# A DeltaNet layer: decays computed ahead of the keys, Q's norms read back from DRAM, gates stored from another queue, one exponential per head

## The chip, the core and the metric

The kernel runs on one core of one Trainium2 chip. Its time is device microseconds for one execution; lower is better. One profiled execution of the same program gives the page and the trace that are quoted below.

## What is computed

A two-layer decoder trunk on 528 tokens (16 meta tokens and 512 real ones) of width 1024, in float32: a retention layer, a SwiGLU feed-forward layer, a gated DeltaNet layer and another feed-forward layer, each with a norm ahead of it and a residual addition. The change touches the DeltaNet layer alone. Its core, for each of 8 heads (chunk by chunk):

```python
qkv = silu(causal_conv(h @ w_in, conv_w))          # 4 taps
q = l2norm(q) * DN_DK ** -0.5;  k = l2norm(k)
beta = sigmoid(beta_in);  g = -exp(a_log) * softplus(a_in + dt_bias)
gam = cumsum(g)                                    # inside a chunk
decay = exp(where(i >= j, gam_i - gam_j, -inf))
a_mat = where(i > j, beta * (k @ k.T) * decay, 0)
u, w = solve(eye + a_mat, [v * beta, k * beta * exp(gam)])
v_new = u - w @ state
o = (q * exp(gam)) @ state + ((q @ k.T) * decay) @ v_new
state = state * exp(g_last) + (k * exp(g_last - gam)).T @ v_new
out = (rmsnorm(o) * silu(gate)) @ w_out
```

## The kernel before

Matrix products keep float32 accuracy by splitting both operands into a rounded high part and a remainder: `hi*hi + hi*lo + lo*hi`, three matmuls for one (`mm3`, L470). A weight block of 128x1024 is loaded by SyncE's queue (`wraw`, L173), its high part is cast by ScalarE (`whi`, L179), and the remainder is formed by VectorE (`wlo`, L180). `gemm` multiplies one such block with all 528 tokens: 48 matmuls of 128x264 into one of two accumulator tiles `g` (two PSUM banks each). Smaller products use four one-bank tiles `m`.

The program is written in one thread of Python with a clock of its own: `tick()` advances it by one step after each k-block of a gemm (six matmuls), and generators that were given to `spawn` with a delay are resumed between matmuls when their step has come; `yield n` asks to be resumed n steps later, `next(gen)` and `finish(gen)` run one at once. The order in which each engine's queue then holds its instructions is set when the program is built. It follows the program's order by priority, but an instruction that is planned to be ready earlier can go ahead of one written before it. On the chip each queue runs in that fixed order.

The DeltaNet layer (`deltanet`, from about 780 us) has these stages:

- Head 0's two key/query gemms (`gemm_pair`), with the row norms `rb` made meanwhile.
- `dn_gates` (L1213): 32 matmuls with the 16 columns of beta and a (L1235, 48 rows of output because of the splitting), ten small transposing matmuls (L1252), a chain of small VectorE and ScalarE operations for beta and softplus, cumulative sums (L1292), and the matrix of decays. For each pair of heads, `rows_in` broadcasts the sums from DRAM into `dec`, GpSimd adds a mask of 1e30 (L1356), and ScalarE takes `exp(-x + sum)` of each 128x128 chunk, four for a head (L1363). It yields between parts (`GATE_STEPS`, `ROWS_IN`, `MASKED`).
- `dn_keys` for each head (L1366): a gemm for K and one for Q. `conv_evac` (L1198) multiplies by `rb` into one of two `pad` buffers (VectorE, L1202), takes the four taps (ScalarE L1205, VectorE L1207), and a Silu (L1210). The result is stored to DRAM (`d_kq`) and split into `z`. For Q, `dn_norms` is spawned: four transposes (L1396), four squares with a row sum (ScalarE, L1400), one small operation (L1402).
- `dn_attention` for each head: K'K and K'Q products, beta and decay applied (L1446), stored to `d_mp`. It needs its pair's decays, and runs `dn_gates` on until they are there.
- `dn_inverse`: forward substitution on VectorE for all heads together, while TensorE multiplies value weights (`dn_values`) and two heads' gate weights (`dn_silu_gate`).
- `dn_states`: the recurrence, pair by pair, among the remaining value, gate and output gemms. The silu'd gates are stored to DRAM (`d_sg`, L1608) and read back when their head is finished (L1695).

ScalarE's Exp and Silu are in different tables; the trace shows an `ACT_TABLE_LOAD` wherever one follows the other.

Of the kernel before, what the change touches and what calls it, by code (L numbers as in the profile page):

```python
# [10 lines left out]
AF = mybir.ActivationFunctionType  # L11
ALU = mybir.AluOpType
PSUM = bass.MemoryType.PSUM

P = 128
D = 1024
KT = D // P
NM = 16
NT = 512
T = NM + NT  # L20
HH = T // 2
EPS = 1e-6

RH = 4
DH = 8
# [18 lines left out]
TO_ATTEND = 7  # L44
ROWS = 5
POW = 5
NORMS = 18
ATTEND = 13
ATTEND_LAST = 8
ROWS_IN = (2, 10)  # L50
PAIRS_APART = 14
MASKED = 4
VALUES = 6
GATE_STEPS = (3, 6, 3)
GATES = [2, 2, 0, 2]
# [4 lines left out]
class Hybrid:  # L60
# [1130 lines left out]
    def conv_silu(self, w, x, rb, mt):  # L1191

        nc = self.nc
        p = self.psum_g()
        self.gemm(p, w, x, range(KT))
        return self.conv_evac(p, rb, mt)

    def conv_evac(self, p, rb, mt):  # L1198
        nc = self.nc
        self.pads.reverse()  # L1200
        pad = self.pads[0]
        nc.vector.tensor_tensor(self.halves(pad[:, 3 : 3 + T]), p[:, :, :HH], self.halves(rb), op=ALU.mult)  # L1202
        acc = self.t(self.tp, [P, T], "ra", bufs=4)
        cw = self.convw
        nc.scalar.activation(acc, pad[:, :T], AF.Copy, scale=cw[:, mt, 0:1])  # L1205
        for i in range(1, 4):
            nc.vector.scalar_tensor_tensor(  # L1207
                acc, pad[:, i : i + T], cw[:, mt, i : i + 1], acc, op0=ALU.mult, op1=ALU.add
            )
        nc.scalar.activation(acc, acc, AF.Silu)  # L1210
        return acc

    def dn_gates(self, sp, x, rb):  # L1213


        nc, a = self.nc, self.a
# [11 lines left out]
        pick = self.t(gp, [48, 16], "pick")  # L1228
        nc.vector.tensor_copy(pick, self.ident[:48, :16])
        nc.vector.tensor_copy(pick[32:48], self.ident[32:48, 32:48])  # L1230
        p = self.psum_g()
        for kt in range(KT):
            for i in range(2):
                for half in range(2):
                    nc.tensor.matmul(  # L1235
                        p[:48, half, :HH],
                        wst[:, kt, :],
                        x[i][:, kt, half * HH : half * HH + HH],
                        start=kt == 0 and i == 0,
                        stop=kt == KT - 1 and i == 1,  # L1240
                    )
        ba = self.t(self.tp, [P, T], "ra", bufs=4)[:48]
        nc.vector.tensor_tensor(self.halves(ba), p[:48, :, :HH], self.halves(rb[:48, :]), op=ALU.mult)
        bm = self.t(self.tp, [P, 96], "am", bufs=1)
        nc.gpsimd.memset(bm, 0.0)
        self.spread(bm[:48], ba[:, :NM])
# [1 line left out]
        pt = self.psum_m()  # L1248
        for ch in range(5):
# [5 lines left out]
        ax, xa, e, z, z2, q = (  # L1255
            tmp[:, 80 + 40 * i : 120 + 40 * i].rearrange("p (a b) -> p a b", b=DH) for i in range(6)
        )
# [38 lines left out]
        sums = self.t(sp, [P, P], "kl")  # L1296
# [4 lines left out]
        pt = self.psum_m()  # L1301
# [6 lines left out]
        def rows_in(pair):  # L1308
            for hd in (2 * pair, 2 * pair + 1):
                self.dec[hd] = self.t(sp, [P, 4, P], ("zh", "zl")[pair % 2], bufs=3)  # L1310
                nc.sync.dma_start(self.dec[hd], by_head[hd, 1:].unsqueeze(0).to_broadcast([P, 4, P]))
# [5 lines left out]
        for dst, mat, meta in ((self.eglast, self.ones, self.ones[:NM, :]), (self.ekw, self.later, later3)):  # L1317
# [14 lines left out]
            op=ALU.mult,  # L1332
# [13 lines left out]
        for pair in range(DH // 2):  # L1346
            hds = (2 * pair, 2 * pair + 1)
            if pair == 1:
                yield PAIRS_APART
            if pair > 0:  # L1350
                while self.attended < 2 * (pair - 1):
                    yield 1
                rows_in(pair)
            yield ROWS_IN[pair > 0]
            for hd in hds:
                nc.gpsimd.tensor_tensor(  # L1356
                    self.dec[hd], self.dec[hd], apart.unsqueeze(1).to_broadcast([P, 4, P]), op=ALU.add
                )
            yield MASKED
            for hd in hds:  # L1360
                for c in range(4):
                    o, de = (c + 1) * DH + hd, self.dec[hd][:, c]
                    nc.scalar.activation(de, de, AF.Exp, scale=-1.0, bias=sums[:, o : o + 1])  # L1363
            self.decays = 2 * pair + 2

    def dn_keys(self, pool, hd, x, rb, first, gt):  # L1366

        nc, a = self.nc, self.a
        for s, base in ((1, 0), (0, 8)):
            if first is None:  # L1370
                w = self.load_w(a["w_dqk"][hd, 1 - s])
                p = self.psum_g()
                self.gemm(p, w, x, range(KT))
            else:
                p = first.pop(0)
            t_ = self.conv_evac(p, rb, base + hd)
            real = t_[:, NM:].rearrange("p (c i) -> p c i", c=4)
            nc.sync.dma_start(self.d_kq[:, hd, :, s, :], real)
            if s == 1:
                zz = self.t(pool, [P, 2, 4, 2, P], "z", F32R)  # L1380
                zh, zl = zz[:, 0], zz[:, 1]
            self.split(zh[:, :, s, :], zl[:, :, s, :], real)
            if s == 0:
                nc.vector.tensor_copy(self.kmf[:, hd, :], t_[:, :NM])
            else:
                self.spawn(self.dn_norms(hd, t_), NORMS)
        return self.spawn(
            self.dn_attention(pool, hd, zh, zl, gt), ATTEND if hd < DH - 1 else ATTEND_LAST
        )

    def dn_norms(self, hd, t_):

        nc = self.nc
        pt = self.psum_m()
        for c in range(4):
            nc.tensor.transpose(pt[:, c * P : (c + 1) * P], t_[:, NM + c * P : NM + (c + 1) * P], self.ident)  # L1396
        eq = self.eq[:, hd, :]
        for c in range(4):
            jk = self.t(self.sp, [P, P], "rh")
            nc.scalar.activation(jk, pt[:, c * P : (c + 1) * P], AF.Square, accum_out=eq[:, c : c + 1])  # L1400
        yield 1
        nc.vector.tensor_scalar(eq, eq, EPS, EPS * P, op0=ALU.add, op1=ALU.mult)  # L1402

    def dn_attention(self, pool, hd, zh, zl, gt):

# [192 lines left out]
    def dn_silu_gate(self, hd, x, rb):  # L1598

        nc, a = self.nc, self.a  # L1600
        p = self.psum_g()
        ws = [self.load_w(a["w_dg"][hd, i]) for i in range(2)]
        for i in range(2):
            self.gemm(p, ws[i], x, range(KT), lo=NM, bank=i)
        sg = self.t(self.gp, [P, 2, NT], "sg", bufs=2)
        nc.vector.tensor_tensor(sg, p, rb[:, NM:].unsqueeze(1).to_broadcast([P, 2, NT]), op=ALU.mult)
        nc.scalar.activation(sg, sg, AF.Silu)
        nc.sync.dma_start(self.d_sg[:, hd], sg)  # L1608

    def dn_scan(self, hd, z, vs, sp):  # L1610

# [152 lines left out]
    def deltanet(self, st, ctx, nxt):  # L1764
        nc, a = self.nc, self.a
        x = (st["hi"], st["lo"])
        self.gp = gp = self.pool(ctx, "dn", 1)
        self.sp = sp = self.pool(ctx, "scan", 2)
        op = self.pool(ctx, "og", 1)
# [26 lines left out]
        def gate(n):  # L1796
            for _ in range(n):
                self.dn_silu_gate(next(gates), x, rb)
# [7 lines left out]
        first = [self.psum_g() for i in range(2)]  # L1806
        self.gemm_pair(first, ws, x)
        self.finish(rows)
        rb = st["rb"]
        gt = self.spawn(self.dn_gates(sp, x, rb))  # L1810
        for hd in range(DH):
            att = self.dn_keys(sp, hd, x, rb, first if hd == 0 else None, gt)
            if hd in KEY_GATES:
# [1 line left out]
        self.dn_values(0, x, rb, sp)  # L1815
        self.finish(att)
        inv = self.spawn(self.dn_inverse(sp))
        self.dn_values(1, x, rb, sp)
        gate(FIRST_GATES)
        self.finish(inv)  # L1820
        self.spawn(self.dn_states(sp, op))
        for pair in range(4):
            gate(GATES[pair])
# [264 lines left out]
```

## Time and profile before

| | |
|---|---|
| median of 3 runs | 1669.75 us (1668.28 to 1670.8) |
| the profiled execution | 1669.76 us, span of its instructions 1668.0 us |
| TensorE matmul busy | 1643.1 us (99%) |
| VectorE busy | 1297.6 us (78%) |
| ScalarE busy | 886.1 us (53%) |
| mean granted TensorE clock | 0.996 |

Times in the trace count from the first instruction of the span. Busy shares are means over stages that differ: in the DeltaNet layer VectorE and ScalarE are much busier than these figures. In a line of the timeline stand: start, length, engine, source line, operation, written tile <- read tiles, shapes, count of merged instructions, and in brackets the engine's idle time before it with what ended it. `PEld` is the loading of weights into TensorE; a `q` behind an engine's name is its DMA queue or sequencer.

### The profile page before, as it was taken

How to read it: one execution, taken by the hardware profiler on the slowest of the kernel's cores; microseconds unless marked ns; L12 is line 12 of the kernel's file. 1: busy time of each engine (PE TensorE's matmuls, PEld its weight loads, DVE VectorE, ACT ScalarE, POOL GpSimd, SP SyncE). 2: the span in 40 equal slices, each digit the busy share in tenths (PEclk: the TensorE clock that was granted, in tenths of full speed). 3: DMA queues.
4: the chain of work that ended last, by engine and by line, in shares of the span. 5: the costliest groups of instructions: out<-in, count | busy, mean ns of one | idle time of the engine just before them, and what ended most of it. 6: DMA issues, size and time to landing. Idle time of an engine off the chain costs nothing.

```text
span 1668.0 us, 30777 instructions
## 1 busy us (share of the span) xinstructions
PE 1643.1 (99%) x12415; PEld 1550.9 (93%) x12415; DVE 1297.6 (78%) x2121; ACT 886.1 (53%) x1536; POOL 99.7 (6%) x139
## 2 busy tenths in 40 slices
PE   9999999999999999999989999999999999999998
PEld 9999999999999999999989988888877889999896
DVE  7886877798698887784689888796876798888672
ACT  5445555555345545543595427776663455555542
POOL 1000000000000000000030000010100000000010
PEclk9999999999999999999999999999999999999999
DMA  6564746565323332453354554432323223333451
GB/s 211 175 165 119 219 111 198 176 210 167 113 89 102 102 102 82 122 155 101 102 158 159 140 143 139 156 104 89 107 75 114 90 89 113 102 107 110 114 163 52
DMA packets 91888, 214.54 MB, mean 129 GB/s; under 512 B 20394, under 2 KB 42146, under 8 KB 90466
## 3 DMA queue, kind: packets, MB, share of 16 engines
q1 hardware_dynamic: 80066, 194.21, 35.3%
q0 software_dynamic: 4688, 16.53, 5.7%
q10 hardware_dynamic: 6992, 1.85, 0.5%
q8 instruction: 97, 1.59, 0.4%
q14 instruction: 45, 0.37, 0.1%
HBM read 190.30 MB, written 22.25 MB: 127 GB/s over the span
## 4 chain that ended last, share of the span: by engine, by line
PE 86%; DVE 9%; ACT 3%; issue 2%; POOL 1%; POOLq 0%; ACTq 0%; DVEq 0%
PE g L470 66%; PE m L470 14%; DVE wlo L461 1%; ACT whi L460 1%; DVE wsum L220 1%; DVE ra L1207 1%; PE m L573 0%; DVE flt L461 0%; POOL ss L1686 0%; PE m L559 0%; PE m L704 0%; DVE wlo L180 0%; DVE wraw L312 0%; DVE flb L461 0%; PE m L143 0%
## 5 line engine op out<-in xcount | busy, mean ns | idle before, releaser
L460 ACT CAST whi<-wraw 128x1024 fp32r<-128x1024 f32 x171 | 179.2, 1051 | 192.5 <-PE g L470 69.4
L470 PE MATMUL g<-fht,whi 128*128 128x264 f32 (+1 forms) x976 | 277.4, 284 | 0.8 <-DVE h L338 0.7
L470 PE MATMUL g<-fht,wlo 128*128 128x264 f32 (+1 forms) x976 | 276.1, 283 | 0.8 <-DVE wlo L461 0.8
L470 PE MATMUL g<-flt,whi 128*128 128x264 f32 (+1 forms) x976 | 275.9, 283 | 0.0
L470 PE MATMUL g<-xlo,whi 128*128 128x264 f32 (+1 forms) x1088 | 260.9, 306 | 0.0
L470 PE MATMUL g<-xhi,whi 128*128 128x264 f32 (+1 forms) x1024 | 251.8, 310 | 4.6 <-ACT whi L179 4.0
L470 PE MATMUL g<-xhi,wlo 128*128 128x264 f32 (+1 forms) x1024 | 251.2, 308 | 2.3 <-DVE wlo L180 2.3
L461 DVE TENSOR_TENSOR wlo<-wraw,whi 128x1024 fp32r<-128x1024 f32 x171 | 210.5, 1234 | 46.5 <-ACT whi L460 46.2
L179 ACT CAST whi<-wraw 128x1024 fp32r<-128x1024 f32 (+3 forms) x117 | 118.1, 1011 | 138.5 <-PE g L470 107.1
L470 PEld LDWEIGHTS g<-fht,whi 128*128 128x128 f32 x976 | 183.8, 188 | 1.3 <-ACT ra L540 0.9
L470 PEld LDWEIGHTS g<-fht,wlo 128*128 128x128 f32 x976 | 183.6, 188 | 1.1 <-DVE wlo L461 1.0
L470 PEld LDWEIGHTS g<-flt,whi 128*128 128x128 f32 x976 | 183.7, 188 | 0.5
L470 PEld LDWEIGHTS g<-xlo,whi 128*128 128x128 f32 x1088 | 176.7, 189 | 7.0 <-DVE xlo L529 0.2
L470 PEld LDWEIGHTS g<-xhi,whi 128*128 128x128 f32 x1024 | 167.8, 190 | 12.4 <-ACT whi L179 4.2
L470 PEld LDWEIGHTS g<-xhi,wlo 128*128 128x128 f32 x1024 | 167.3, 189 | 10.1 <-DVE wlo L180 3.3
L180 DVE TENSOR_TENSOR wlo<-wraw,whi 128x1024 fp32r<-128x1024 f32 (+3 forms) x117 | 138.0, 1180 | 40.5 <-ACT whi L179 39.5
L470 PE MATMUL g<-fhb,whi 128*128 128x264 f32 (+1 forms) x480 | 137.4, 286 | 0.0
L470 PE MATMUL g<-fhb,wlo 128*128 128x264 f32 (+1 forms) x480 | 136.1, 284 | 1.0 <-DVE wlo L461 0.8
L470 PE MATMUL g<-flb,whi 128*128 128x264 f32 (+1 forms) x480 | 135.7, 283 | 0.0
L461 DVE TENSOR_TENSOR wlo<-wsum,whi 128x1024 fp32r<-128x1024 f32 x54 | 66.1, 1225 | 44.5 <-ACT whi L460 44.5
L470 PEld LDWEIGHTS g<-fhb,wlo 128*128 128x128 f32 x480 | 90.3, 188 | 1.8 <-DVE wlo L461 1.8
L470 PEld LDWEIGHTS g<-flb,whi 128*128 128x128 f32 x480 | 90.3, 188 | 0.5
(562 smaller groups left out, 3804.4 us busy)
## 6 DMA issues: line engine op xcount, KB each, us to landing
wraw<-in_w_gu_dram SPq DMA_DIRECT2D x66, 512.0 KB, 3.4
wraw<-in_w_ret_dram SPq DMA_DIRECT2D x56, 512.0 KB, 3.7
sraw<-in_w_gu_dram SPq DMA_DIRECT2D x22, 512.0 KB, 4.1
wraw<-in_w_ret_dram POOLq DMA_DIRECT2D x18, 512.0 KB, 5.6
wraw<-in_w_dqk_dram SPq DMA_DIRECT2D x16, 512.0 KB, 3.4
wraw<-in_w_dv_dram SPq DMA_DIRECT2D x16, 512.0 KB, 3.3
wraw<-in_w_dg_dram SPq DMA_DIRECT2D x16, 512.0 KB, 3.9
wraw<-in_w_do_dram SPq DMA_DIRECT2D x16, 512.0 KB, 3.4
```

The lines of the kernel that those rows point to most:

```text
L179: nc.scalar.copy(hi[:, c], raw[:, c])
L180: nc.vector.tensor_tensor(lo[:, c], raw[:, c], hi[:, c].bitcast(F32), op=ALU.subtract)
L220: nc.vector.scalar_tensor_tensor(dst[:, k, :], hh[:, kb + k, cs], g[:, kb + k : kb + k + 1], rb[:, cs], op0=ALU.mult, op1=ALU.mult)
L460: self.nc.scalar.copy(hi, src)
L461: self.nc.vector.tensor_tensor(lo, src, hi.bitcast(F32), op=ALU.subtract)
L470: mm(o, l, r[which], start=first and n == 0, stop=last and n == 2, **kw)
L1207: nc.vector.scalar_tensor_tensor(acc, pad[:, i : i + T], cw[:, mt, i : i + 1], acc, op0=ALU.mult, op1=ALU.add)
```

## The change

Five things change in the code.

1. The first two parts of `dn_gates` run before the first `dn_keys`, without steps between them; the third is spawned 6 steps later. Its 32 matmuls write two `m` tiles in place of one `g` tile, and are evacuated by two operations. Both of head 0's gemm results are evacuated into the two pads (`conv_pad`) ahead of it; the taps (`conv_taps`) follow in `dn_keys`.
2. `dn_norms` becomes one generator for all heads, spawned with `dn_inverse`. It loads Q of each head from `d_kq`, two heads ahead, and transposes and squares it, a head every five steps.
3. The gate's store to `d_sg` is issued from ScalarE's queue in place of SyncE's.
4. The four exponentials of a head become four Identity activations with the same scale and bias, in place, and one Exp over the head's 128x512 follows.
5. The wait of 4 steps (`MASKED`) between mask and exponentials goes; 2 steps (`RAISED`) stand between the Identities of a pair and its two exponentials.

The diff, shortened:

```diff
-NORMS = 18
-MASKED = 4
+RAISED = 2
+NORMS = 4
 def dn_gates(self, sp, x, rb):
-        p = self.psum_g()
+        p = [self.psum_m()[:48, :HH] for half in range(2)]
...
-        nc.vector.tensor_tensor(self.halves(ba), p[:48, :, :HH], self.halves(rb[:48, :]), op=ALU.mult)
+        for half in range(2):
+            hs = slice(half * HH, half * HH + HH)
+            nc.vector.tensor_tensor(ba[:, hs], p[half], rb[:48, hs], op=ALU.mult)
...
-            yield MASKED
             for hd in hds:
                 for c in range(4):
                     o, de = (c + 1) * DH + hd, self.dec[hd][:, c]
-                    nc.scalar.activation(de, de, AF.Exp, scale=-1.0, bias=sums[:, o : o + 1])
+                    nc.scalar.activation(de, de, AF.Identity, scale=-1.0, bias=sums[:, o : o + 1])
+            yield RAISED
+            for hd in hds:
+                nc.scalar.activation(self.dec[hd], self.dec[hd], AF.Exp)
 def dn_keys(self, pool, hd, x, rb, first, gt):
...
-            else:
-                self.spawn(self.dn_norms(hd, t_), NORMS)
+    def dn_norms(self, sp):
+        nc = self.nc
+        def load(hd):
+            q = self.t(sp, [P, 4, P], "zh", bufs=3)
+            nc.sync.dma_start(q, self.d_kq[:, hd, :, 1, :])
+            return q
+        qs = [load(hd) for hd in range(2)]
+        for hd in range(DH):
+            yield NORMS
+            q = qs.pop(0)
+            if hd + 2 < DH:
+                qs.append(load(hd + 2))
+            pt = self.psum_m()
+            for c in range(4):
+                nc.tensor.transpose(pt[:, c * P : (c + 1) * P], q[:, c], self.ident)
+            eq = self.eq[:, hd, :]
+            for c in range(4):
+                jk = self.t(self.sp, [P, P], "rh")
+                nc.scalar.activation(jk, pt[:, c * P : (c + 1) * P], AF.Square, accum_out=eq[:, c : c + 1])
+            yield 1
+        nc.vector.tensor_scalar(self.eq, self.eq, EPS, EPS * P, op0=ALU.add, op1=ALU.mult)
 def dn_silu_gate(self, hd, x, rb):
-        nc.sync.dma_start(self.d_sg[:, hd], sg)
+        nc.scalar.dma_start(self.d_sg[:, hd], sg)
 def deltanet(self, st, ctx, nxt):
-        gt = self.spawn(self.dn_gates(sp, x, rb))
+        first = [self.conv_pad(p, rb) for p in first]
+        gt = self.dn_gates(sp, x, rb)
+        for _ in range(2):
+            next(gt)
+        self.spawn(gt, GATE_STEPS[1])
...
         inv = self.spawn(self.dn_inverse(sp))
+        norms = self.spawn(self.dn_norms(sp))
         self.dn_values(1, x, rb, sp)
         gate(FIRST_GATES)
         self.finish(inv)
+        self.finish(norms)
```

More of the change, by code (lines that the diff above doesn't have):

```diff
@@ L1195, in conv_silu, with conv_pad, conv_taps @@
         self.gemm(p, w, x, range(KT))
-        return self.conv_evac(p, rb, mt)
-    def conv_evac(self, p, rb, mt):
-        nc = self.nc
+        return self.conv_taps(self.conv_pad(p, rb), mt)
+    def conv_pad(self, p, rb):
         self.pads.reverse()
         pad = self.pads[0]
-        nc.vector.tensor_tensor(self.halves(pad[:, 3 : 3 + T]), p[:, :, :HH], self.halves(rb), op=ALU.mult)
+        self.nc.vector.tensor_tensor(self.halves(pad[:, 3 : 3 + T]), p[:, :, :HH], self.halves(rb), op=ALU.mult)
+        return pad
+    def conv_taps(self, pad, mt):
+        nc = self.nc
         acc = self.t(self.tp, [P, T], "ra", bufs=4)
@@ L1235, in dn_gates @@
                     nc.tensor.matmul(
-                        p[:48, half, :HH],
+                        p[half],
                         wst[:, kt, :],
@@ L1371, in dn_keys @@
                 w = self.load_w(a["w_dqk"][hd, 1 - s])
-                p = self.psum_g()
-                self.gemm(p, w, x, range(KT))
-            else:
-                p = first.pop(0)
-            t_ = self.conv_evac(p, rb, base + hd)
+                t_ = self.conv_silu(w, x, rb, base + hd)
+            else:
+                t_ = self.conv_taps(first.pop(0), base + hd)
             real = t_[:, NM:].rearrange("p (c i) -> p c i", c=4)
@@ L1389, in dn_keys @@
         )
-    def dn_norms(self, hd, t_):
+    def dn_norms(self, sp):
         nc = self.nc
[L1394 to L1402, printed above, removed]
+        def load(hd):
[17 more added lines that the diff above has]
+        nc.vector.tensor_scalar(self.eq, self.eq, EPS, EPS * P, op0=ALU.add, op1=ALU.mult)
     def dn_attention(self, pool, hd, zh, zl, gt):
```

## The prediction

> **What bounds the kernel now.** First the page's busy times: TensorE is busy for 99% of the span, so only TensorE work that disappears, or time in which it stands or runs slowly, can shorten the kernel.
>
> ```profile
> span 1668.0 us, 30777 instructions
> PE 1643.1 (99%) x12415; PEld 1550.9 (93%) x12415; DVE 1297.6 (78%) x2121; ACT 886.1 (53%) x1536; POOL 99.7 (6%) x139
> ```
>
> The change touches the DeltaNet layer only (about 800 to 1330 us), and removes no matmul. So I asked who made TensorE wait there, from 800 to 1400 us, then took busy times by stretch: keys and attention products (802 to 938), inverses (938 to 1001), and two cuts around the one long wait.
>
> ```profile
> PE g L470 <- ACT whi L179: 4.0, 1, 4.0
> PE g L470 <- DVE wlo L180: 2.3, 3, 1.4
> ...
> PE m L1424 <- DVE km L616: 1.0, 1, 1.0
> ...
> PE g L470 <- DVE pad L1202: 0.6, 1, 0.6
> ```
>
> ```profile
> core 0: us, PE busy (x) PEld busy (x) DVE busy (x) ACT busy (x) POOL busy (x), PEclk, DMA share, GB/s
> 802.00:938.00 136.00, 129.44 (x1046) 127.36 (x1046) 119.46 (x310) 92.08 (x192) 22.66 (x18) 0.97 0.47 146
> 938.00:1001.00 63.00, 61.55 (x332) 52.43 (x331) 50.26 (x125) 23.24 (x32) 0.00 (x0) 1.00 0.56 143
> 846.00:866.00 20.00, 14.31 (x113) 13.47 (x112) 17.96 (x48) 19.21 (x35) 4.06 (x3) 1.00 0.33 107
> 848.00:873.00 25.00, 18.59 (x124) 17.44 (x124) 21.81 (x53) 24.15 (x47) 2.51 (x3) 0.86 0.43 126
> 873.00:938.00 65.00, 65.00 (x542) 65.00 (x541) 58.03 (x162) 33.48 (x75) 7.94 (x6) 1.00 0.47 158
> ```
>
> (The first lines read: who waited, for whom, us in all, times, longest. The others: stretch, length, busy us and instructions of each engine, granted clock, DMA share, GB/s.) Nearly all the loss of the key stretch lies in 848 to 873: 25 us with 18.59 busy, 6.41 idle, at a mean clock of 0.86. After it TensorE runs 65 of 65 us. ScalarE explains the place: 19.21 of 20 us busy. The matmuls in order of time show the long wait and what follows it:
>
> ```profile
> 866.17 0.81 PE L470 MATMUL g<-xhi,whi 128*128 128x264 f32 x2 [3.99 <-ACT whi L179]
> ...
> 867.97 0.81 PE L470 MATMUL g<-xhi,wlo 128*128 128x264 f32 x2 [0.55 <-DVE wlo L180]
> ...
> 872.88 0.40 PE L470 MATMUL g<-xlo,whi 128*128 128x264 f32 x2
> 873.12 0.40 PE L470 MATMUL g<-xhi,wlo 128*128 128x264 f32 x2
> ```
>
> Each line is a pair of matmuls. After the 3.99 us wait, thirteen pairs take 872.88 - 866.17 = 6.71 us; at the 0.24 us a pair of the last two lines they need 3.1, and 0.55 of the rest is the wait shown, so 3.0 us is the slow clock. The other 6.41 - 3.99 = 2.4 us of idleness are the small waits for VectorE listed above (the 1.4 of wlo is another place, at 998 us). The place costs 6.4 + 3.0 = 9.4 us.
>
> ScalarE's own order shows what held the weight cast (L179) that ends the long wait:
>
> ```profile
> 847.53 1.28 ACT L1363 ACT_TABLE_LOAD   x1
> 848.83 0.70 ACT L1363 ACTIVATE zh<-zh,kl 128x128 f32<-128x128 f32 x2
> 849.54 1.28 ACT L1210 ACT_TABLE_LOAD   x1
> 850.84 0.65 ACT L1210 ACTIVATE ra<-ra 128x528 f32<-128x528 f32 x1
> ...
> 865.08 1.04 ACT L179 CAST whi<-wraw 128x1024 fp32r<-128x1024 f32 x1
> ```
>
> The eight exponentials of pair 2, written consecutively in the code, are spread among the convolutions' Silus; each alternation loads a table twice, 1.28 us each. By line, in 846 to 866, ScalarE spent on decays (L1363), Silus (L1210) and norms (L1400):
>
> ```profile
> 846.00:866.00 20.00, 6.52 (x11) 1.00 0.33 107
> 846.00:866.00 20.00, 5.79 (x6) 1.00 0.33 107
> 846.00:866.00 20.00, 1.13 (x8) 1.00 0.33 107
> ```
>
> 11 instructions are three loads and eight exponentials, 6 are three loads and three Silus: six loads, 7.7 of 20 us.
>
> **The change part by part.**
>
> *Decays.* Each of 32 exponentials becomes an Identity of the same shape and operands; I take the same time (a pair's eight cost 6.52 - 3 x 1.28 = 2.7 us). One Exp of 128x512 for each head is added; the nearest row is the 128x512 cast:
>
> ```profile
> L460 ACT CAST z<-ra 128x512 fp32r<-128x512 f32 x16 | 9.8, 610 | 0.2
> ```
>
> So +1.2 us a pair. Identity must need no table, like the Copy at L1205 and the Square at L1400, which run behind either table with no load of their own. Instead of eight places where a Silu can come between, a pair has two, adjacent in code: two loads if they stay together, four if not, against six here.
>
> *Norms.* The squares (1.13 us in this stretch) leave ScalarE. The sum for 846 to 866: together, -5.1 - 1.1 + 1.2 = -5.0 us; apart, -2.6 - 1.1 + 1.2 = -2.5 us. The 865.08 cast comes that much earlier, so the 3.99 wait shrinks by 2.5 to 3.99; I take 3.4, near the middle.
>
> *Clock.* With 3.4 gone, 0.6 us of gap remains, 1.5 at worst. The nearest short gap and the rows behind it:
>
> ```profile
> 998.67 0.51 PE L470 MATMUL g<-xhi,wlo 128*128 128x264 f32 x2 [1.44 <-DVE wlo L180]
> 999.02 0.40 PE L470 MATMUL g<-xhi,whi 128*128 128x264 f32 x2
> 999.26 0.40 PE L470 MATMUL g<-xlo,whi 128*128 128x264 f32 x2
> ```
>
> 1.44 us of idleness left the pace at 0.24 a pair. So I take all 3.0 us of slow clock (bounds 0 and 3.0). The traces do not show what a gap between 1.44 and 3.99 does. The Trainium skill ("TensorE: Matmul & The Clock Gate", "Why this matters for your kernels") says gaps over about 3 us return TensorE to half rate; by it, a remaining gap of up to 3 would also keep the 3.0 us.
>
> *The small waits* (2.4 us) end with VectorE, busy 119.46 of 136 us, whose work hardly changes: it loses seven of eight small L1402 operations and evacuates the gates in two pieces. Less delay from ScalarE helps it; taps postponed behind the gates' chain hurt it. Bounds 0 and 2.4; I take 1.2.
>
> *Beta and decays first.* The 32 gate matmuls and ten transposes are the same work. They leave the two-buffer g accumulators for m, both of head 0's results are evacuated at once, and the chain starts some microseconds earlier. Both pads are then full: the third evacuation waits for head 0's first taps. Two free accumulators, a gemm of 48 matmuls at 0.12 us each, cover 11.6 us. I take 0; without that cover the third evacuation would block TensorE for about the gates' VectorE chain, some 5 us.
>
> *Transposes.* A set of four, and the pair behind it:
>
> ```profile
> 846.66 0.60 PE L1396 MATMUL m<-ident,ra 128*128 128x128 f32 x4
> 847.02 0.49 PE L470 MATMUL g<-xhi,whi 128*128 128x264 f32 x2
> ```
>
> Eight sets of 0.36 us, 2.9 us, leave the keys and come back among the inverses, where TensorE is 61.55 of 63 us busy: 0, bounds -1.4 (filling idle time) and 0. The squares land where ScalarE is 23.24 of 63 us busy: 0.
>
> *Reading Q back.* Eight loads of 256 KB join SP's queue, two ahead. DMA share there is 0.56. A step of the code's clock, six matmuls, is 0.73 us; a transpose set stands five steps behind the previous, so the lead is 2.9 us for head 0, 6.5 for head 1, some 10 steps (7.2 us) later. Times to landing, and what SP waits for from 940 to 1400:
>
> ```profile
> d_kq<-ra SPq DMA_DIRECT2D x16, 256.0 KB, 2.4
> zh<-d_g SPq DMA_DIRECT2D x4, 256.0 KB, 6.0
> ```
>
> ```profile
> SPq L173 <- DVE wlo L180: 150.9, 21, 18.5
> SPq L1608 <- ACT sg L1607: 40.0, 6, 10.6
> ```
>
> At 6.0 us only head 0 is late, by 3.1 us; at 2.4 none is. Other ready matmuls may go ahead: I take +0.5, bounds 0 and 3.1.
>
> *Gate stores.* SP loses 40.0 us of waiting, but no TensorE wait from 800 to 1400 us ends with a weight's DMA: 0. ScalarE gains eight issues; on SP one takes 0.33 us:
>
> ```profile
> L1608 SPq DMA_DIRECT2D d_sg<-sg x8: 319/326/990, 959.9 to 1262.2; - x8
> ```
>
> Each waits for its Silu to finish, and ScalarE's next casts queue behind it. Bounds 0 and 2.6 us, +0.3 taken, as ScalarE has idle time around the gates.
>
> Sum: -3.4 - 3.0 - 1.2 + 0.5 + 0.3 = -6.8 us. The profiled execution took 1669.76 us, equal to the median, 1669.75. Forecast 1663.0 us.
>
> One row weighs against a page: the load at 847.53 ends at 848.81 and the exponential starts at 848.83, so a switch costs 1.30 us. The Trainium skill ("ScalarE: Activation LUTs", "What ACT_TABLE_LOAD costs") adds a drain of 1.38 us to the 1.28; the trace has no room for it. By the page's 2.66 the saved switches would free 5.3 to 10.6 us, the whole 3.99 would go in either case, and the sum would be -7.4, 1662.4 us.
>
> **The rivals.**
>
> B: the thrash stays. If head-by-head Exps meet Silus in other places, or other stretches take the loads, the gap stays above 3 us and the clock falls. Only a microsecond is left of the gain: about 1668.8 us. For it: eight adjacent exponentials were split three ways. Against: two chances to split remain in a pair, and the squares leave anyway.
>
> C: VectorE takes over. The key stretch shortens by 9.4 at most to 126.6 us against 119.46 of VectorE work, 94%; in 873 to 938 TensorE holds full speed with VectorE at 58.03 of 65, 89%. If the slow clock goes but the long wait turns into VectorE waits (POOL's mask additions still fall in this stretch): -3.0 - 0.5 + 0.3 = about 1666.5 us.
>
> D, slower: Q's reads come late. They share SP's queue with weight loads that wait for a buffer, 150.9 us in 21 waits, 7.2 us each; a read behind one takes 7.2 + 2.4 = 9.6 against a lead of 7.2, and TensorE's queue stands at the transposes 2.4 us, eight times: 19 us against 7.3 won elsewhere, 1681.7 us. It decides from a mean wait of (7.3 + 3.3)/8 = 1.3 us. Against: one such wait in a row of eight, with other matmuls placed in between, is likelier than eight.
>
> **How the numbers follow.** 0.2% is 3.3 us, about what a measurement of this kernel can tell from no change: faster is below 1666.4, slower above 1673.1. Forecast 0.62, its own range 1659 (9.4 and the 1.4 all won) to 1666.4; C 0.12, half of it faster; B 0.13, same; D 0.13, slower. So 0.68, 0.19, 0.13. The range runs from 1658 to 1672 us: it takes in B and C and leaves D and a little of each side out.
>
> **What would show it.** In the changed trace: Exp loads in the key stretch fewer, in two to four per pair; Identities without loads; ScalarE below 19 of 20 us around pair 2; no TensorE wait over 1.5 us between 840 and 870 and the clock at 1.00; the waits for whi gone. Q's transposes at 935 to 970 without waits, SP's waits at the gate stores gone. The prediction is wrong if a wait of 3 us or more stands anywhere in the layer, if Identity loads a table, or if TensorE waits at Q's transposes.

## The result, and the profile after

The changed kernel is slower: a median of 1691.59 us (1690.41 to 1693.38), against 1670.28 for the kernel before; ratio 1.0122, 95% interval 1.0109 to 1.0134. The forecast was 1663.0. Below, `A` is the kernel before and `B` the changed one; in `B` the lines of the code have other numbers (the Silu is L1213, the Identity L1367, the new Exp L1370, the cast `um` L1521, the weight cast still L179).

The head of `B`'s page and TensorE's waits in it from 800 to 1400 us (who waited for whom, us in all, times, longest):

```profile
span 1689.8 us, 30770 instructions
PE 1654.0 (98%) x12415; PEld 1560.2 (92%) x12415; DVE 1297.9 (77%) x2115; ACT 881.9 (52%) x1538; POOL 102.4 (6%) x139
```

```profile
PE g L470 <- ACT whi L179: 11.3, 2, 7.7
PE m L1439 <- DVE km L616: 4.1, 2, 3.9
PE m L1541 <- DMA z<-d_mp: 2.1, 1, 2.1
```

TensorE's busy time grew by 11 us with the same 12415 matmuls: part of them ran slowly, and the other 11 us of the longer span are idle time. Cuts of `B` through the two places, then the same cuts of `A` (columns as in the prediction):

```profile
840.00:860.00 20.00, 16.26 (x110) 16.05 (x111) 16.82 (x43) 15.81 (x33) 6.74 (x5) 0.83 0.43 130
860.00:880.00 20.00, 16.36 (x110) 15.85 (x109) 16.63 (x34) 14.95 (x24) 3.49 (x2) 0.83 0.54 175
...
980.00:1000.00 20.00, 16.69 (x86) 13.24 (x84) 12.51 (x47) 3.43 (x7) 0.00 (x0) 1.00 0.72 164
1000.00:1020.00 20.00, 13.52 (x125) 12.09 (x126) 5.78 (x11) 8.86 (x21) 0.00 (x0) 0.50 0.63 212
```

```profile
840.00:860.00 20.00, 18.14 (x147) 17.53 (x146) 18.15 (x46) 17.53 (x35) 6.22 (x5) 1.00 0.45 137
860.00:880.00 20.00, 15.45 (x105) 14.91 (x104) 15.38 (x34) 18.28 (x36) 2.45 (x2) 0.83 0.51 148
...
980.00:1000.00 20.00, 18.56 (x111) 16.29 (x109) 13.11 (x41) 6.21 (x7) 0.00 (x0) 1.00 0.65 133
1000.00:1020.00 20.00, 20.00 (x235) 18.83 (x234) 15.12 (x33) 14.45 (x38) 0.00 (x0) 1.00 0.71 245
```

In the keys `B` has two places at 0.83 of the clock where `A` has one. Where the inverses end, at 1000 to 1020 us, `A` works 20 of 20 us at full clock; `B` works 13.52 at half of it. To say how much each place costs, two marks are used for every run: the start of the store of head 7's products (`d_mp`, end of the keys) and the last update of `h` in the layer. `A` has them at 936.7 and 1312.5 us, `B` at 938.3 and 1334.1: 1.6 us late after the keys, 21.6 late at the end. It was 1.5 us late already at the start of the keys (the first evacuation there, at 804.07 against 802.59). **So about 20 us are lost behind the keys, and the keys themselves, where all of the gain was forecast, gave nothing.**

TensorE, then ScalarE, where `B`'s inverses end:

```profile
998.14 0.65 PE L1541 MATMUL m<-wl,z 32*64 32x32 f32 x16 [2.11 <-DMA z<-d_mp]
1006.48 0.81 PE L470 MATMUL g<-xhi,whi 128*128 128x264 f32 x2 [7.68 <-ACT whi L179]
```

```profile
997.33 1.06 ACT L1622 ACTIVATE sg<-sg 128x1024 f32<-128x1024 f32 x1 [6.02 <-DVE sg L1621]
997.39 0.34 ACTq L1623 DMA_DIRECT2D d_sg<-sg  x1
997.83 0.42 ACTq L1520 DMA_DIRECT2D rr<-d_m  x1
...
1005.02 0.30 ACT L1521 CAST um<-rr 96x128 fp32r<-96x128 f32 x1 [5.50 <-DMA rr<-d_m]
1005.38 2.94 ACT L179 CAST whi<-wraw 128x1024 fp32r<-128x1024 f32 x3
```

and the same place in `A`:

```profile
992.25 1.06 ACT L1607 ACTIVATE sg<-sg 128x1024 f32<-128x1024 f32 x1 [9.56 <-DVE sg L1606]
993.21 1.03 ACT L179 CAST whi<-wraw 128x1024 fp32r<-128x1024 f32 x1
997.68 0.32 ACTq L1505 DMA_DIRECT2D rr<-d_m  x1
998.16 1.99 ACT L179 CAST whi<-wraw 128x1024 fp32r<-128x1024 f32 x2
1004.42 0.30 ACT L1506 CAST um<-rr 96x128 fp32r<-96x128 f32 x1 [1.78 <-DMA rr<-d_m]
```

The cast `um` needs a small matrix that has gone to DRAM and is read back by three reads (`rr`). Two are issued from SyncE's queue, in `B` at 994.59 and 995.09; the third, from ScalarE's queue, goes out only at 997.83 and lands last. How long the three took from issue to landing in `B`:

```profile
DMA to landing us min/median/max: 3.4/3.7/7.1
```

`um` starts 7.2 us after the issue of the third read in `B`, 6.7 in `A`. What the third read would take from SyncE's queue was not tried. In `A` three weight casts stand ahead of `um` in ScalarE's queue; in `B` all three stand behind it. TensorE, through with the last gate at 996.0, has only sixteen small matmuls (998.14) to do until the first of them is made. The Trainium skill ("PSUM — Partial Sum Buffer", "Engine vs sequencer instructions") says that ScalarE's queue is strictly first in, first out. The casts at 1005.38 agree: with `um` moved to another engine (um_on_gpsimd, below) the same three run at 997.36, so it was only their place that held them.

### The profile page after: what moved, and what is told of

Same layout as the page of the kernel before. It is cut to its first block, busy times and chain, and to the rows that moved or that the text cites. A ratio compares the mean times of both kernels' runs of the same rounds, so it can differ in the third digit from the quotient of the medians.

```text
span 1689.8 us, 30770 instructions
## 1 busy us (share of the span) xinstructions
PE 1654.0 (98%) x12415; PEld 1560.2 (92%) x12415; DVE 1297.9 (77%) x2115; ACT 881.9 (52%) x1538; POOL 102.4 (6%) x139
## 4 chain that ended last, share of the span: by engine, by line
PE 81%; DVE 11%; ACT 3%; issue 3%; DMA 2%; POOL 1%; SPq 0%; ACTq 0%; POOLq 0%; DVEq 0%
PE g L470 62%; PE m L470 14%; DVE wlo L461 2%; ACT whi L460 1%; DVE wraw L312 1%; DMA wraw<-in_w_ret_dram 1%; DVE wsum L220 1%; POOL ss L1701 1%; DVE flt L461 0%; DVE ra L596 0%; PE m L559 0%; DMA rr<-d_m 0%; DMA h<-in_hT_dram 0%; PE m L573 0%; PE m L1605 0%
## 5 line engine op out<-in xcount | busy, mean ns | idle before, releaser
L470 PE MATMUL g<-xhi,whi 128*128 128x264 f32 (+1 forms) x1024 | 255.3, 313 | 11.4 <-ACT whi L179 11.3
L470 PEld LDWEIGHTS g<-fht,whi 128*128 128x128 f32 x976 | 183.8, 188 | 1.6 <-ACT ra L540 1.1
L179 ACT CAST whi<-wraw 128x1024 fp32r<-128x1024 f32 (+3 forms) x117 | 118.0, 1011 | 122.7 <-PE g L470 96.3
```

What stands on the lines that cost most here:

```text
L179: nc.scalar.copy(hi[:, c], raw[:, c])
L470: mm(o, l, r[which], start=first and n == 0, stop=last and n == 2, **kw)
```

## The experiments

Theory Q: the order of ScalarE's queue at `um` is the loss. Theory N: it is Q's norms among the inverses. Theory K: it is the key stretch. For each run: its ratio to the kernel before, then how late (+) it passes the start of the keys and the two marks against `A`, in us.

| run | ratio (95%) | start of keys | end of keys | end of layer | between the marks |
|---|---|---|---|---|---|
| `B` | 1.0122 (1.0109–1.0134) | +1.5 | +1.6 | +21.6 | +20.0 |
| undo_store | 1.0047 (1.0034–1.0059) | +0.9 | +0.4 | +8.7 | +8.3 |
| undo_norms | 1.0024 (1.0015–1.0033) | 0.0 | +1.8 | +4.5 | +2.7 |
| undo_gates | 1.0083 (1.0071–1.0096) | +0.2 | -5.3 | +12.7 | +18.0 |
| undo_exp | 1.0042 (1.0029–1.0054) | 0.0 | -11.8 | +7.1 | +18.9 |
| um_on_gpsimd | 1.0105 (1.0090–1.0121) | +0.9 | -0.6 | +15.7 | +16.3 |
| um_all_gpsimd | 1.0062 (1.0050–1.0074) | +1.2 | +0.3 | +13.0 | +12.7 |
| wait_before_identities | 1.0085 (1.0072–1.0098) | +1.1 | -4.3 | +14.7 | +19.0 |
| gates_alone | 0.9989 (0.9980–0.9998) | +1.4 | -0.9 | -1.2 | -0.3 |
| norms_alone | 0.9993 (0.9984–1.0002) | -0.3 | -9.8 | +0.3 | +10.1 |
| exp_alone | 1.0002 (0.9993–1.0011) | +1.2 | +2.4 | +1.0 | -1.4 |
| store_alone | 1.0009 (1.0001–1.0018) | +2.9 | +1.4 | +2.6 | +1.2 |
| no_norms | 0.9933 (0.9918–0.9949) | +0.3 | -11.1 | -11.1 | 0.0 |
| norms_in_states | 0.9978 (0.9968–0.9989) | +0.1 | -10.3 | -3.5 | +6.8 |
| norms_in_states_gates | 0.9973 (0.9960–0.9987) | +0.9 | -11.0 | +0.5 | +11.5 |
| norms_with_merge | 0.9972 (0.9954–0.9990) | +1.0 | -10.0 | -5.5 | +4.5 |
| norms_in_scan_gates | 0.9980 (0.9969–0.9991) | +1.4 | -9.8 | -3.9 | +5.9 |

The marks come from one profiled execution each, which lies within 2.3 us of its run's median. "Start of keys" is the first evacuation there; it is drift from ahead of the layer, so what the keys themselves cost is the end of the keys less their start. What is said below of the keys is reckoned so.

**One part undone.**

```diff
 # undo_store
-        nc.scalar.dma_start(self.d_sg[:, hd], sg)
+        nc.sync.dma_start(self.d_sg[:, hd], sg)
 # undo_norms: dn_norms as before, four transposes and squares in each head's keys
-        norms = self.spawn(self.dn_norms(sp))
+                self.spawn(self.dn_norms(hd, t_), NORMS)
 # undo_gates: gates spawned as before, in one g tile
-        first = [self.conv_pad(p, rb) for p in first]
+        gt = self.spawn(self.dn_gates(sp, x, rb))
 # undo_exp: four exponentials with bias for a head, behind MASKED
-            yield RAISED
+            yield MASKED
```

> The changed kernel with the gate stores back on SyncE's queue. Theory Q (the order of ScalarE's queue): the loss sits behind the inverses, where ScalarE's fixed order in the changed kernel has the cast `um` (it waits for a round trip through DRAM) ahead of three weight casts, and TensorE waits 2.1 + 7.7 us and then runs some 10 to 15 us at half its clock. With the store on SyncE's queue the three casts stand ahead of `um`. So the wait of 7.7 us goes, and with it the slow clock: between the kernel before plus what was lost at the last inverse store (1.6 us) and plus what was lost at the gates (5.1 us), 1672 to 1676 us. Theory N (Q's norms among the inverses are what starves TensorE): 1686 to 1692. Theory K (the key stretch): 1688 to 1692.

> The changed kernel with Q's norms back in the key stretch. Theory Q: the store on ScalarE's queue still puts `um` ahead of weight casts, but of two in place of three, so TensorE has one gemm more in hand (48 matmuls of 0.12 us, 5.8 us): the wait of 7.7 shrinks to about 2, and the half clock may go or stay: 1672 to 1682 us, a wait for `whi` after `um` still to be seen near 1000 us. Theory N: the norms are the whole cause, 1665 to 1670. Theory K: 1686 to 1692.

> The changed kernel with beta and the decays begun as before (not ahead of the keys). Theories Q and N: the order behind the inverses is untouched, 1687 to 1694 us; the first pair's decays come later by about 1.6 us. Theory K, with the early gates as its cause: 1680 or less, and the wait of 3.9 us for `km` near 843 us gone.

> The changed kernel with one exponential with bias for each chunk, as before, in place of Identity and one exponential per head. Theories Q and N: 1687 to 1694 us. Theory K, with the blocks of Identity and exponential as its cause: 1680 or less, and the waits of 3.9 and 3.6 us in 840 to 866 smaller.

Undoing the store wins 11.7 of the 20 us behind the keys, undoing the norms 17.3, the other two 1 to 2. In undo_store the three casts are ahead of `um` again, as Q had said, but 8.3 us stay lost, and its time, 1678.54 us, is above Q's range. What is left there stands in norms_alone too (below), with the same wait of 3.39 us: it is the norms' own. TensorE's wait, and the slow cut behind it, are

```profile
998.06 0.51 PE L470 MATMUL g<-xhi,whi 128*128 128x264 f32 x2 [3.39 <-ACT whi L179]
```

```profile
1000.00:1020.00 20.00, 19.99 (x209) 18.24 (x208) 9.62 (x21) 10.37 (x30) 0.00 (x0) 0.84 0.56 203
```

Q and N both hold in part. undo_norms, with the store still changed, has one of the three casts behind `um`, and `um` itself has nothing left to wait for when its turn comes: near 1000 us TensorE waits 1.45 us, as in `A`, and not the 2 us for `whi` that Q had expected. Theory K was wrong on the place of the loss but right that the exponentials cost: undo_exp's keys are 11.9 us shorter than `B`'s. undo_gates, at 1684.52 us, came between the ranges.

**One part alone.** The same edits, added one at a time to `A`.

> The kernel before with beta and the decays ahead of the keys, nothing else. Theory G: the early start of the decays alone removes the stall of the key stretch (9 to 12 us, as it stood 11.8 us ahead at head 7's products when gates and norms were moved and the exponentials were as before), and behind the inverses the order is that of before: 1658 to 1662 us. Theory S: the stall goes only if the squares leave ScalarE as well: 1667 to 1672.

> The kernel before with Identity and one exponential per head, nothing else. Theory Bk (blocks): a pair's eight Identities and its exponentials stand in one piece ahead of the Silus and weight casts, and a wait of 3 us or more for `km` or `whi` stands between 840 and 870 us: 1671 to 1684. Theory T (the prediction's: fewer table loads free ScalarE): no such wait, 1661 to 1667.

> The kernel before with Q's norms read back among the inverses, nothing else. Theory N2: the stretch behind the inverses loses about 9.8 us, as it does with the store on SyncE's queue (a wait for `whi` of about 3.4 us, a slow clock behind it, 3.5 us of transposes), and the keys win 2 to 6: 1674 to 1679. Theory Q alone (only the store does harm): 1664 to 1670.

> The kernel before with the gate stores on ScalarE's queue, nothing else. Theory Q: the store puts `um` ahead of two weight casts even without the norms, but TensorE has more work in hand there; with gates, exponentials and store changed and the norms left, this place lost 2.9 us: 1671 to 1677 us, with a wait for `whi` or `wlo` near 1000 us. Rival (the store costs only together with the norms): 1668 to 1671, no wait over 1.5 us near 1000.

Alone none moves the time by as much as 0.2%. Theory G fell: the early gates win 2.3 us in the keys, not 9. The stall stays, as S had said, but by another engine: the wait for `whi` is gone, and one as long for `pad` stands in its place, behind VectorE, which is busy for 13.78 of the 14 us before:

```profile
853.01 0.48 PE L470 MATMUL g<-xhi,whi 128*128 128x264 f32 x2 [4.04 <-DVE pad L1201]
```

Of the exponentials neither theory held in full: the longest waits are 2.6, 1.9 and 1.4 us, none of them the 3 us that Bk asked for, and nothing is gained. store_alone lies in Q's range by its time, but its one wait near 1000 us is the 1.45 of `A`, as the rival said: the store costs only beside the norms. The norms alone do what the whole change was meant to do, 9.5 us in the keys, and lose 10.1 us where they are put, as N2 said; that the time then fell in the range of Q alone is chance. The parts do not add up: between the marks the store costs 1.2 alone, the norms 10.1, and the four together 20.0.

**The wait for `um`.**

```diff
 # um_on_gpsimd
-        nc.scalar.copy(self.um, um)
+        nc.gpsimd.tensor_copy(self.um, um)
 # um_all_gpsimd: also this subtraction, and the two copies of um into u3
-        nc.vector.tensor_tensor(self.um[64:96], um[64:96], self.um[64:96].bitcast(F32), op=ALU.subtract)
+        nc.gpsimd.tensor_tensor(self.um[64:96], um[64:96], self.um[64:96].bitcast(F32), op=ALU.subtract)
```

> The whole change, with the cast `um` on GpSimd in place of ScalarE; the rest of ScalarE's order stays (gate Silu, gate store, copies, then three weight casts). Theory Q: the cast that waits for DRAM is what holds the weight casts, so the wait of 7.7 us for `whi` shrinks to 1 to 2 us (what remains is the copy `rh`, behind a matmul that ends at 998.8 us), and of the slow clock behind it (13.5 us at half speed, 6.7 us lost) some or all goes: 6 to 13 us less than the changed kernel, 1678 to 1686. Theory N: the casts are held by the order in which the inverse's stores and the gates stand, and something else holds them as long: 1688 to 1693.

> The whole change; the cast `um`, the subtraction behind it and the two copies of it into `u3` go to GpSimd, so that neither ScalarE's nor VectorE's queue waits for the round trip through DRAM. With the cast alone on GpSimd, the subtraction on VectorE held the remainders `wlo` for 4.3 us in place of the casts. Theory Q: now that wait goes too, and what stays behind the inverses is what the norms bring (about 10 us): 4 to 9 us under the run with the cast alone moved, 1677 to 1683 us, no wait over 3 us there for `whi` or `wlo`. Theory N (the time lies in the order of gates and stores and comes back elsewhere): 1685 to 1690.

um_on_gpsimd, at 1687.55 us, came between the ranges. With the cast gone from ScalarE, TensorE's waits there were 1.88 for `whi` and then, in um_on_gpsimd,

```profile
1004.76 0.81 PE L470 MATMUL g<-xhi,wlo 128*128 128x264 f32 x2 [4.33 <-DVE wlo L180]
```

because VectorE had the subtraction, which waits for the same read, ahead of the remainders:

```profile
1002.98 0.28 DVE L1522 TENSOR_TENSOR um<-rr,um 32x128 fp32r<-32x128 f32 x1 [7.72 <-POOL um L1521]
...
1003.50 3.47 DVE L180 TENSOR_TENSOR wlo<-wraw,whi 128x1024 fp32r<-128x1024 f32 x3
```

Moved away too (um_all_gpsimd), the loss between the marks falls from 20.0 to 12.7. So 7.3 us are the queues that wait for `um`: theory Q, at about a third of the place. The waits that remain are 2.08 for `z` and 2.60 for `whi`. The 12.7 us stand near norms_alone's 10.1, which fits theory N for the rest; why undoing the store wins 4.4 us more than moving `um` was not taken apart.

**The keys.** The order of ScalarE's queue with one wait back in place:

```diff
 # wait_before_identities
+            yield 4
             for hd in hds:
                 for c in range(4):
```

> The whole change with four steps of waiting between GpSimd's mask and the Identities, as there were before the exponentials. Theory Bk (what costs in the keys is the order that the block of Identities and exponentials gets: some 30 us without a weight cast, which here has one cast and two Silus moved ahead of pair 1's block): the keys end 4 to 10 us earlier, 1681 to 1688 us. Theory W (the 1.2 us a pair of added work, or the table loads, cost it): 1689 to 1694.

The keys are 5.5 us shorter than in `B`, with the same Identities and exponentials. So of the 11.9 us that undo_exp wins there about half is their place alone (Bk); the other half was not separated. How that looks, ScalarE by line from 820 to 880 us (count; busy us, mean ns), in `B` and then in undo_exp:

```profile
L1213 ACT ACT_TABLE_LOAD x5 | 6.4, 1283 | 0.1
L179 ACT CAST whi<-wraw 128x1024 fp32r<-128x1024 f32 x6 | 6.2, 1039 | 5.9 <-PE g L470 5.9
...
L1370 ACT ACT_TABLE_LOAD x3 | 3.8, 1283 | 0.1
```

```profile
L179 ACT CAST whi<-wraw 128x1024 fp32r<-128x1024 f32 x9 | 9.3, 1041 | 3.6 <-PE g L470 3.6
L1213 ACT ACT_TABLE_LOAD x7 | 9.0, 1283 | 0.1
L1368 ACT ACT_TABLE_LOAD x6 | 7.7, 1283 | 0.1
```

Of these two users undo_exp has 13 table loads in the stretch where `B` has 8, and yet 9 weight casts to `B`'s 6, and TensorE's longest wait in the keys is 0.73 us. In `B` no weight cast stands between the one at 832 us and the one at 863:

```profile
832.13 1.05 ACT L179 CAST whi<-wraw 128x1024 fp32r<-128x1024 f32 x1 [3.56 <-PE g L470]
834.14 1.28 ACT L1367 ACTIVATE zh<-zh,kl 128x128 f32<-128x128 f32 x4 [0.96 <-POOL zh L1361]
...
837.63 1.14 ACT L1370 ACTIVATE zh<-zh 128x512 f32<-128x512 f32 x2
838.79 1.28 ACT L1213 ACT_TABLE_LOAD   x1
840.08 0.64 ACT L1213 ACTIVATE ra<-ra 128x528 f32<-128x528 f32 x1
...
862.97 1.03 ACT L179 CAST whi<-wraw 128x1024 fp32r<-128x1024 f32 x1
```

The Silu at 840.08 stood behind pair 0's block, and `km` (TensorE's 3.93 us wait, ending at 843.59) behind that Silu; the cast at 862.97 stood behind pair 2's block, and ended the other wait, 3.63 us. Of the 3.93, about 2 us came after the Silu and go with GpSimd: the two copies that make `km` took 1.17 and 1.21 us on VectorE, where the next ones in `B` take 0.16 and 0.17, and each ended within 0.05 us of a mask addition there:

```profile
841.12 1.17 DVE L1389 COPY kmf<-ra 128x16 f32<-128x16 f32 x1
842.32 1.21 DVE L616 COPY km<-kmf 128x48 f32<-128x48 f32 x1
```

```profile
841.00 1.27 POOL L1361 TENSOR_TENSOR zh<-zh,kh 128x512 f32<-128x512 f32 x1
842.23 1.26 POOL L1361 TENSOR_TENSOR zl<-zl,kh 128x512 f32<-128x512 f32 x1
```

No run moved the mask additions, so this share is read from one place of the trace (and from the same place of wait_before_identities, 1.18 and 1.21), not shown by an experiment.

**Norms left out, and put elsewhere.** All on `A`; the two with "gates" have the early gates too.

```diff
 # no_norms: no transposes, no squares
+        nc.gpsimd.memset(self.eq, 1.0)
 # norms_in_states: per head, from the recurrence's own z, behind dn_merge
+            nc.tensor.transpose(pt[:, c * P : (c + 1) * P], z[:, c, 1, :], self.ident)
...
+        self.dn_norm(hd, z)
+        yield
 # norms_with_merge: the call inside dn_merge's second step, no step of its own
 # norms_in_scan_gates: the call beside the first chunk's own square
```

> The kernel before with Q's norms left out (no transposes, no squares; the sums are set to one, so the output lacks Q's normalisation). It says what of the 10 us that the keys win can reach the end at all. Theory L (later stages keep a lead; with the norms in the recurrence it was the norms' own place that lost it): the 10 us in the keys reach the end, 1657 to 1661 us. Theory C0 (a later stage gives the lead back whatever is done with the norms): 1663 to 1669 us.

> The kernel before with Q's norms taken from `z` in the recurrence, and nothing else. Theory Q+N: the keys win 9.8 us as with the norms among the inverses, 2.9 come back: 1661 to 1665 us. Theory C0: 1667 to 1672.

> Beta and the decays first as in the change, the exponentials and the gate stores as before, and Q's norms taken out of the keys but not put among the inverses: each head's four transposes and squares read Q from the tile `z` that the recurrence loads anyway, behind the head's inverse is merged. Theory Q+N (squares and transposes leaving the keys win about 10 to 12 us there, and only their place among the inverses costs it again): ScalarE's order behind the inverses is again that of before, 2.9 us of transposes come back in the recurrence: 1658 to 1663 us. Theory C0 (what is won in the keys is always given back, because VectorE's inverses or the recurrence set the pace): 1667 to 1672.

> The kernel before with Q's norms taken from `z`, in the first step of the merge of each head's inverse and without a step of their own. Theory L: the step of its own and the place ahead of the scan cost about 5 of the 10 us; here 2.9 us of transposes remain: 1660 to 1664. Theory C0: as with the other place, 1665 to 1669.

> Gates first, and Q's norms taken from `z` beside the first chunk's own square in the recurrence, without a step of their own. Theory L: 1659 to 1663. Theory C0: 1665 to 1669.

no_norms leaves out the norms, and Q's normalisation with them. It settles one question: a lead of 11.1 us out of the keys stands to the end, so nothing later takes it back by itself, and C0 is out. Read from `z`, the norms leave ScalarE's order at `um` as in `A` (no wait over 1.45 us there), but 4.5 to 11.5 us go between the marks, of which the transposes are 2.9 by the prediction's row. All four times lie where C0 had put them, though its reason is out. norms_with_merge is 0.3% faster than the kernel before, and by its lower bound 0.1%; the others are alike within their intervals. Part of the rest is the clock. In norms_in_states it is at 0.50 for 6.8 us from 1062.7, in norms_in_states_gates for 6.8 us from 998.9 and 10.3 from 1063.7, with TensorE busy almost throughout; an estimate of half that time gives 3.4 of the 6.8 us between the marks and 8 of the 11.5 (an execution 2.3 us above its run's median). `A` and the other two runs have the full clock in these places; their rest is open. The early gates brought nothing on top.

## Why the prediction was wrong

Of the sum's -7.6 us in the keys (-3.4 - 3.0 - 1.2) none came, and the two terms behind the keys, +0.8 together, came to +20.0.

- **Shrinking the 3.99 us wait (-3.4): the step that failed first.** The loads fell as forecast and Identity loaded no table; the Exp of 128x512 took 0.62 us, forecast 0.61; ScalarE's busy time in 846 to 866 fell from 19.21 to 15.82 us (below), inside the forecast's 2.5 to 5.0, though the two cuts do not hold quite the same work. But "the 865.08 cast comes that much earlier" does not follow. The cast's time is set by its place in a fixed order; a queue with 13 loads fed TensorE better than one with 8.

```profile
846.00:866.00 20.00, 16.20 (x110) 15.48 (x109) 18.35 (x52) 15.82 (x28) 5.18 (x3) 0.84 0.28 83
```

- **Slow clock (-3.0) and small waits (-1.2).** Nothing won: two waits over 3.6 us in place of one, both with the clock at 0.83. Rival B (the thrash stays) came nearest for the keys, though not by its mechanism. Rival C (VectorE takes over) is to be seen in gates_alone's 4.04 us for `pad`; where the -0.5 us in its sum comes from, the prediction does not say. That a short gap leaves the pace alone was read from one row, and `A`'s own trace holds a place that says otherwise (last section).
- **Norms: squares -1.1, transposes 0: mis-sized in the keys, wrong among the inverses.** The squares were counted in the 20 us around the wait, one head's, 1.13 us. For all eight heads `A` spends 9.76 us of ScalarE on them:

```profile
800.00:940.00 140.00, 9.76 (x64) 0.98 0.46 144
```

  and without them and the transposes the keys are 9.5 to 11.4 us shorter (norms_alone, no_norms). Among the inverses "0, bounds -1.4 and 0" was wrong in sign. From the end of the keys to the fourth gate's evacuation `B` falls back by 3.5 us (1.6 to 5.1), near the 2.9 of the eight transposes; then come waits of 2.11 + 7.68 where `A` has 1.44 (8.4), and 20 us at half clock in which TensorE worked 13.52 (6.8). Together 18.7 of the 20.0.
- **Gate stores (+0.3, bounds 0 and 2.6).** Right alone (1.2 us between the marks, 1.0009), wrong beside the norms: putting them back wins 11.7. I named the danger (ScalarE's casts behind a waiting store) and priced it by idle time, not by what stands in the queue behind it.
- **Beta and decays first (0).** Near enough alone (0.9989). The cover held: in `B` TensorE works 40.00 of 40 us from 780 to 820, so the third evacuation stops nothing. With the other parts in place undoing it won 7 us, 5.6 of them in the keys, where one wait of 4.42 us for `km` stands in place of two; that was not taken further.
- **Q's reads (+0.5) and rival D.** The reads landed 3.3 us after issue, and the transposes waited for none; rival D had the right sign, and the nearest time (1681.7), by the wrong mechanism: luck.
- **SP freed (0).** Right: its waits at the gate stores went, and those at the weight loads grew from 150.9 to 183.8 us.

What the sum lacked is one check: each moved or lengthened operation shifts the plan from which the queues' orders are made, and at one point of ScalarE's queue an instruction waits for a read that takes some 7 us, with three weight casts near it. That place could be seen in the trace before.

## What to carry to other kernels

Where queues run in a fixed order, price a change not by an engine's busy time but by what stands ahead of the instructions that feed the bottleneck, above all near an instruction that waits for a round trip through DRAM; such a cast wants a queue that feeds nobody. Work taken out of a crowded stretch is worth what it unblocks there (here some 10 us on TensorE's path, for 2.9 us of TensorE's work and 9.8 of ScalarE's), and in these runs it kept that worth only as far as its new place left the feeding queue's order and TensorE's pace alone. Parts that are each neutral alone can cost 1.2% together, so time them together before believing any.

## What the runs showed of the hardware

TensorE has two paces in these traces. In undo_norms a single wait of 2.77 us is followed by the slow one:

```profile
849.53 0.81 PE L470 MATMUL g<-xhi,wlo 128*128 128x264 f32 x2 [2.77 <-DVE wlo L180]
850.14 0.64 PE L470 MATMUL g<-xhi,whi 128*128 128x264 f32 x2
850.58 0.64 PE L470 MATMUL g<-xlo,whi 128*128 128x264 f32 x2
...
855.78 0.40 PE L470 MATMUL g<-xlo,whi 128*128 128x264 f32 x2
856.02 0.41 PE L470 MATMUL g<-xhi,wlo 128*128 128x264 f32 x2
```

The pairs come every 0.44 us for some 6 us, then every 0.24. The Trainium skill ("TensorE: Matmul & The Clock Gate", "Why this matters for your kernels") puts the bound at about 3 us of idling. These traces give no bound by the length of one gap. In undo_norms 2.77 was enough; elsewhere less was, and then again it was not. `A` has two gaps close together, and the clock is at 0.50 from 1289.2 to 1292.6 behind them (below them, the cut around the place):

```profile
1286.49 0.73 PE L470 MATMUL g<-oh,whi 128*128 128x512 f32 x2 [1.42 <-ACT oh L460]
1288.12 0.50 PE L470 MATMUL g<-ol,whi 128*128 128x512 f32 x1 [0.90 <-DVE ol L461]
```

```profile
1284.00:1300.00 16.00, 13.68 (x51) 10.36 (x50) 9.16 (x12) 6.52 (x10) 0.00 (x0) 0.89 0.21 71
```

exp_alone has the same two gaps, 1.42 and 0.90 (at 1289.04 and 1290.67), and its clock stays at 1.00 from 1287 to 1303. In norms_in_states the clock falls to 0.50 at 1062.7 although no wait in the 12 us before was over 0.60 us; TensorE was busy for 11.06 of the 12.70 us ahead of it. What decides is not shown. The slow stretches have few lengths: 3.4 us in `A` at 1289.2, 6.8 in `A` at 865.9 and in `B` at 842.9, 20.5 in `B` from 999.9, which begins inside the wait of 7.68 us and has small waits of the merge in it.
